# A decoder trunk's sums of the first gate and up weights formed during the second scan, and loads, casts and stores around the second norm in another order

## The chip, the cores and the metric

One core of a Trainium2 chip. The metric is the device time of one execution in microseconds, the lower the better. The engines are TensorE (PE: matmuls), VectorE (DVE), ScalarE (ACT), GpSimd (POOL) and SyncE (SP, which here only issues DMAs). Each works through its own instructions in program order and waits where an operand is not there yet.

## The reference

One layer of a hybrid decoder on x of 1024 rows by 1024 channels, in fp32:

```python
h = rms_norm(x, norm1_g)
proj = h @ w_in
o_a = gated_deltanet(q, k, v, z, a, b)   # 4 heads x 128, chunks of 64, a scan over the chunks
o_b = multiscale_pool(hp, pool_w, pool_scale)
o_c = short_gated_conv(cb, cc, ch, sconv_w)
x = x + concat(o_a, o_b, o_c) @ w_out
h = rms_norm(x, norm2_g)
ff = silu(h @ w_gate) * (h @ w_up)       # 2816 hidden channels
x = x + ff @ w_down
x = x + sigmoid(x @ ple_gate) * (p @ ple_proj)
return rms_norm(x, final_g)
```

## The kernel before

**Numbers as pairs.** An fp32 operand is split into a high part (a cast to fp32r on ACT) and a low part (operand minus high part, on DVE), and each product is three matmuls: high x high, high x low, low x high. Tiles are transposed: 128 channels on the partitions, 512 of the 1024 rows (a half, `hf`) along the free axis. A unit `u` is 128 x 512 fp32, 256 KB.

**Stages.** The input projection and the delta rule run for two pairs of heads. The scan of the second pair lies between some 260 and 370 us, with matmuls of the last input blocks filled in between its steps. The out-projection follows, half 0 from some 375 and half 1 from some 428 us: eight column blocks of `w_out` each, every block 512 KB, loaded into the buffer `wr`, cast into `wh` (ACT) and `wl` (DVE). For each block `out_evac` (L1233) adds the residual on DVE, squares on ACT, and adds to the sum of squares `ssq2` on DVE. `norm2` (L1266) then takes `rstd` (L457: four small matmuls of `ssq2` with `ones`, the scale `ms` on DVE, the power `rs` on POOL) and `rows` (L471: four diagonals on DVE, one product on PE that spreads them over the partitions), multiplies the tiles and splits them.

**Gate and up.** They are done two column blocks at a time by a Strassen form with seven products, whose right operands are the seven split sets `B[0]` to `B[6]` and whose left operands `op` are splits of weight blocks or of their sums. A sum takes four additions or subtractions for one weight pair. For the first four gemms (`EARLY`) they are made ahead: `early_sums` (L604) loads four units of a weight, makes four results on DVE and stores them in the scratch `sd_d`, from where `weights()` (L1340 and on) loads them later. For the others `sums(n)` (L1399) does it on POOL. `product` (L1470) runs the twelve matmuls of one product.

**Embedding.** `p_proc` (L1490) loads and splits the per-layer input `pT`, `embed` (L1512) multiplies it with `ple_proj` in sixteen banks of six matmuls, between the first products of gate and up, and `embed_evac` (L1504) copies each bank on ACT and stores it in the scratch `pp_d`, which is read at the end of the kernel.

**What sets the order.** A planner, `Flow` (L28), keeps modelled times. Each step is a generator that yields an event, a delay or both, and is resumed when the modelled time has come; what it then emits is appended to its engine's queue. Events and delays in the code thus fix the order of each engine's instructions, not when they run. `calm` lets a step wait until a modelled engine is nearly free. `op_slots` holds back the casts of `op`.

Of the kernel before, what the change touches and what calls it, by code (L numbers as in the profile page):

```python
# [24 lines left out]
EARLY = 4  # L25
# [171 lines left out]
def kernel(  # L197
# [19 lines left out]
    fl = Flow()  # L217
# [12 lines left out]
    pp_d = scr.tile([2, KT, P, HALF], F32, name="pp_d")  # L230
# [31 lines left out]
    def store(dst, src, ev):  # L262

        sync.dma_start(out=dst, in_=src)
        ev.set(2.6)
        yield 0
# [335 lines left out]
    sd_ev = [Event(fl) for _ in range(EARLY)]  # L602

    def early_sums():  # L604
        yield in_done[1], 8.0
        raw = []

        def fetch(n):
            raw.append([load(w[:, r]) for w in gate_up(n) for r in (slice(0, 4), slice(4, 8))])

        fetch(0)
        yield 5.0
        for n in range(EARLY):
            if n + 1 < EARLY:
                fetch(n + 1)
            a11, a12, a21, a22 = raw.pop(0)
            s1 = unit(shape=(P, 4, P))
            for out, in0, in1, op in ((s1, a21, a22, ALU.add), (a21, a11, a21, ALU.subtract),
                                      (a11, s1, a11, ALU.subtract), (a12, a12, a11, ALU.subtract)):
                yield from fl.calm(9, "vec", slack=0.5)  # L620
                vec.tensor_tensor(out=out, in0=in0, in1=in1, op=op)
            yield fl.left() + 1.0
            for i, t in enumerate((a11, a21, s1, a12)):
                sync.dma_start(out=sd_d[n, i // 2, :, 4 * (i % 2):4 * (i % 2) + 4], in_=t)
            a11 = a12 = a21 = a22 = s1 = t = None
            sd_ev[n].set(3.0)


    def conv_evac(tap, dst, ready):
# [359 lines left out]
    in_done = events(2)  # L989
# [239 lines left out]
    def xl_load(n):  # L1229
        if n < 2 * KT:  # L1230
            xl_.append(load(xT[n % KT, :, half(n // KT)]))
# [32 lines left out]
        B_ev[i][k].set(fl.left())  # L1264

    def norm2(hf, ts):  # L1266
        yield x1_ev[hf], 1.0 + 1.5 * hf
        rs = yield from rstd(ssq2[hf])
        ps = yield from rows(rs, unit())
        yield 0.3  # L1270

        def normed(j):
            t = ts[hf][j] = unit()
            vec.scalar_tensor_tensor(out=t, in0=x1[hf][j], scalar=vt[:, V_N2 + j:V_N2 + j + 1], in1=ps,
                                     op0=ALU.mult, op1=ALU.mult)
            x1[hf][j] = None
            return t

        if hf == 0:
            for j in range(KT):  # L1280
                t = normed(j)
                fl.spawn(b_split(j // 4, j % 4, t, vec), fl.left())
                yield fl.lag("vec")
            return
        T1, T2 = [None] * 4, [None] * 4
        for k in range(4):
            t12, t22 = normed(k), normed(4 + k)
            T1[k], T2[k] = unit(), unit()
            vec.tensor_tensor(out=T1[k], in0=t12, in1=ts[0][k], op=ALU.subtract)
            yield fl.lag("vec")  # L1290
            vec.tensor_tensor(out=T2[k], in0=t22, in1=T1[k], op=ALU.subtract)
            ts[0][k] = None
            fl.spawn(b_split(2, k, T2[k], vec), fl.left())
            yield fl.lag("vec")
        t2_ev.set()
        for k in range(4):
            t = ts[1][k]
            vec.tensor_tensor(out=t, in0=ts[1][4 + k], in1=t, op=ALU.subtract)
            fl.spawn(b_split(3, k, t, vec), fl.left())
            ts[1][k] = None  # L1300
            yield fl.lag("vec")
        for k in range(4):
            fl.spawn(b_split(4, k, T1[k], vec))
            T1[k] = None
            yield fl.lag("vec")
        for k in range(4):
            fl.spawn(b_split(5, k, ts[1][4 + k], vec))
            ts[1][4 + k] = None
            yield fl.lag("vec")
        b22_ev.set()  # L1310
        for k in range(4):
            t = ts[0][4 + k]
            vec.tensor_tensor(out=t, in0=t, in1=T2[k], op=ALU.subtract)
            fl.spawn(b_split(6, k, t, vec), fl.left())
            T2[k] = ts[0][4 + k] = None
            yield fl.lag("vec")
        t4_ev.set()
# [33 lines left out]
    def weights():  # L1351
# [45 lines left out]
                    yield 0.1  # L1397

        def sums(n):  # L1399
            yield raws[n][2]  # L1400
            yield raws[n][3]
            ra, rb = raws[n][0:2]
            a11, a12, a21, a22 = ra[:, 0:4], ra[:, 4:8], rb[:, 0:4], rb[:, 4:8]
            s1 = unit(shape=(P, 4, P))
            pool.tensor_tensor(out=s1, in0=a21, in1=a22, op=ALU.add)
            pool.tensor_tensor(out=a21, in0=a11, in1=a21, op=ALU.subtract)
            own[n] = (a11, a12, a11, a21, s1, a12, a22)
            yield split_ev[n]
            pool.tensor_tensor(out=a11, in0=s1, in1=a11, op=ALU.subtract)
            pool.tensor_tensor(out=a12, in0=a12, in1=a11, op=ALU.subtract)  # L1410
            yield fl.left()
            sum_ev[n].set()
# [77 lines left out]
    def p_proc(hf):  # L1490
        def ph():
            return unit(F32R) if hf else ffp.tile([P, HALF], F32R, tag="ph", name=nm("ph"), bufs=4)

        pH[hf] = [[ph() for _ in range(2)] for _ in range(2)]
        raw = [load(pT[k, :, half(hf)]) for k in range(2)]
        yield 4.0
        for k in range(2):
            hi, lo = pH[hf][k]
            act.copy(out=hi, in_=raw[k])
            yield fl.lag("act")  # L1500
            vec.tensor_tensor(out=lo, in0=raw[k], in1=hi.bitcast(F32), op=ALU.subtract)
            pH_ev[hf].set(fl.left())

    def embed_evac(ps, hf, j):  # L1504
        t = unit()
        act.copy(out=t, in_=ps)
        act.dma_start(out=pp_d[hf, j], in_=t)  # L1507
        free(ps)
        pp_ev[hf][j].set(4.0)
        yield 0  # L1510

    def embed(hf):  # L1512
        fl.until(pH_ev[hf])
# [125 lines left out]
    def down_sums(p, units=False):  # L1639
# [20 lines left out]
        if not units:  # L1660
            rb_slots.give()
            rb_slots.give()

    xl_load(0)
    ts2 = [[None] * KT, [None] * KT]
    for hf in range(2):
        fl.until(mix_done[hf])
        if hf == 1:
            ph1.close()
            ff = ctx.enter_context(ExitStack())  # L1670
            ffp = ff.enter_context(tc.tile_pool(name="ffp", bufs=2))
        fl.spawn(norm2(hf, ts2))
        for j in range(KT):
            w = wts.next()
            wts.prepare()
            if hf == 1 and j == 1:
                fl.spawn(weights())
                fl.spawn(p_proc(0), 12.0)
            ps = gemm(w, [mix[hf][k] for k in MIX_ORDER])
            fl.spawn(out_evac(ps, j, hf), 0.3)  # L1680
            if hf == 1 and j == KT - 2:
                out_w.set()
                for _ in range(4):
                    op_slots.give()


    x2 = [[None] * KT, [None] * KT]
# [48 lines left out]
            fl.spawn(down_sums(p), 2.0)  # L1736

    g = [t[1] for t in todo]
    fl.spawn(p_proc(1))
    for n in range(0, EARLY, 2):  # L1740
        for f in (Gemm.head1, Gemm.head2):
            f(g[n])
# [233 lines left out]
```

## Time and profile before

| | us |
|---|---|
| three runs | 1249.65, 1250.87, 1255.29 |
| median | 1250.87 |
| the profiled execution | 1251.02 |
| its span | 1249.2 |
| PE busy | 1214.4 (97%) |
| DVE busy | 812.4 (65%) |
| ACT busy | 530.3 (42%) |
| POOL busy | 295.3 (24%) |
| PE's mean granted clock | 0.991 |

Times in the trace count from the start of the span, which is 1.8 us shorter than the profiled execution. The granted clock is a share of the full 2.4 GHz; 0.50 is the lower of its two levels, 1.2 GHz. In a timeline, the bracket gives how long the engine idled before an instruction and what it had waited for, so the instruction's start less that time is where the wait began. L141 and L349 are helpers through which nearly all instructions of DVE, ACT and PE pass. The tile names are what tells them apart: `mm` and `dn` are banks of PSUM, `wr` raw weights, `wh`, `wl`, `op` split weights, `u` everything else of 128 x 512. The scratch `x1_d` appears as `x_d`.

### The profile page before, as it was taken

Reading aid. Unit: us, or ns where it says so; the run is one execution under the profiler, and the core shown is the slowest. Engines: PE = TensorE matmul, PEld = TensorE weight load, DVE = VectorE, ACT = ScalarE, POOL = GpSimd, SP = SyncE. Lnnn points to the kernel's source line nnn. Section 1 sums busy time; section 2 is a strip of 40 time slices with the busy share of each in tenths; the row PEclk is TensorE's granted clock in tenths of the full one; section 3 lists DMA queues with packets and bytes.
Section 4 is the critical chain, followed back from the end, with each engine's and each line's share of the span. In section 5 each row is a group of like instructions: output and inputs, shape, how many; then the busy total and the mean of one; then the engine's idle time right before and its main releaser. Section 6 shows DMA issues by size and latency. Waiting matters only on the chain.

```text
span 1249.2 us, 17275 instructions
## 1 busy us (share of the span) xinstructions
PE 1214.4 (97%) x6103; PEld 1002.4 (80%) x6103; DVE 812.4 (65%) x1397; ACT 530.3 (42%) x1114; POOL 295.3 (24%) x241
## 2 busy tenths in 40 slices
PE   8999999999999998999999999999999999999996
PEld 6778888888887776777888888888888888888886
DVE  8576785985767677685455657565655865553674
ACT  7255453244234243643333333333344644443553
POOL 7100001100010001013444658655733000000001
PEclk8999999999999999999999999999999999999998
DMA  6046353342245984543333546545569966563452
GB/s 224 18 136 188 110 132 98 108 110 86 86 158 205 325 288 152 181 157 110 110 110 127 177 136 223 180 134 171 177 227 375 323 221 199 178 194 112 147 181 94
DMA packets 119143, 208.18 MB, mean 167 GB/s; under 512 B 24400, under 2 KB 39568, under 8 KB 119056
## 3 DMA queue, kind: packets, MB, share of 16 engines
q1 hardware_dynamic: 116752, 202.88, 49.6%
q10 hardware_dynamic: 2304, 4.20, 0.9%
q8 instruction: 48, 0.79, 0.3%
q14 instruction: 39, 0.32, 0.1%
HBM read 148.53 MB, written 58.49 MB: 166 GB/s over the span
## 4 chain that ended last, share of the span: by engine, by line
PE 73%; DVE 5%; DMA 5%; ACT 3%; issue 2%; ACTq 0%; SPq 0%; POOL 0%; POOLq 0%; DVEq 0%
PE dn L349 44%; PE mm L349 28%; DVE u L141 3%; DMA wr<-in_w_out_dram 2%; ACT u L141 2%; PE dn L703 1%; DVE wl L141 1%; DVE op L141 1%; DMA wr<-in_ple_gate_dram 1%; DMA wr<-in_w_gate_dram 1%; ACT wh L141 1%; DMA sd_d<-u 1%; ACT op L141 0%; ACTq L1507 0%; DMA u<-in_pT_dram 0%
## 5 line engine op out<-in xcount | busy, mean ns | idle before, releaser
L349 PE MATMUL dn<-u,op 128*128 128x512 f32 x1632 | 375.4, 390 | 7.3 <-ACT u L141 4.2
L349 PEld LDWEIGHTS dn<-u,op 128*128 128x128 f32 x1632 | 305.9, 188 | 73.0 <-ACT u L141 5.5
L349 PE MATMUL mm<-u,wh 128*128 128x512 f32 x1104 | 356.4, 403 | 7.0 <-DVE u L141 5.7
L141 DVE TENSOR_TENSOR u<-u,u 128x512 fp32r<-128x512 f32 (+2 forms) x376 | 251.6, 702 | 63.7 <-ACT u L141 57.5
L349 PEld LDWEIGHTS mm<-u,wh 128*128 128x128 f32 x1104 | 202.9, 190 | 52.6 <-DVE u L141 8.4
L349 PE MATMUL mm<-u,wl 128*128 128x512 f32 x552 | 218.0, 395 | 0.9 <-DVE wl L141 0.9
L141 DVE TENSOR_TENSOR op<-wr,op 128x512 fp32r<-128x512 f32 x144 | 134.2, 936 | 104.1 <-ACT op L141 103.0
L141 ACT CAST u<-u 128x512 fp32r<-128x512 f32 x216 | 127.2, 621 | 139.1 <-DVE u L141 44.4
L349 PE MATMUL dn<-u,u 128*128 128x512 f32 (+2 forms) x850 | 159.4, 336 | 0.0
L349 PEld LDWEIGHTS dn<-u,u 128*128 128x128 f32 (+1 forms) x850 | 123.6, 170 | 24.0 <-issue 0.5
L141 ACT CAST op<-wr 128x512 fp32r<-128x512 f32 x144 | 88.4, 620 | 106.2 <-PE dn L349 60.3
L141 POOL TENSOR_TENSOR u<-u,u 128x512 f32<-128x512 f32 (+1 forms) x69 | 99.3, 1453 | 111.7 <-DVE u L141 80.5
L349 PEld LDWEIGHTS mm<-u,wl 128*128 128x128 f32 x552 | 104.8, 190 | 24.9 <-DVE wl L141 2.6
L141 ACT ACTIVATE u<-u 128x512 f32<-128x512 f32 (+1 forms) x137 | 82.1, 605 | 87.5 <-DVE u L141 86.0
L349 PE MATMUL mm<-u,u 128*128 128x512 f32 (+1 forms) x522 | 111.7, 351 | 2.1 <-DVE u L141 1.4
L141 DVE TENSOR_TENSOR wl<-wr,wh 128x512 fp32r<-128x512 f32 (+2 forms) x96 | 68.4, 714 | 65.2 <-ACT wh L141 64.5
L141 ACT COPY u<-dn 128x512 f32<-128x512 f32 (+4 forms) x99 | 47.7, 482 | 134.2 <-PE dn L349 121.1
L141 DVE TENSOR_TENSOR u<-dn,u 128x512 f32<-128x512 f32 x93 | 63.6, 688 | 58.5 <-PE dn L349 56.9
L349 PEld LDWEIGHTS mm<-u,u 128*128 128x128 f32 x522 | 85.5, 189 | 16.3 <-DVE u L141 2.0
L141 POOL TENSOR_TENSOR rs<-ms,mhalf 128x4 f32<-128x4 f32 (+1 forms) x7 | 7.0, 997 | 351.0 <-DVE ms L141 351.0
L141 ACT CAST wh<-wr 128x512 fp32r<-128x512 f32 (+2 forms) x96 | 57.7, 608 | 31.7 <-DMA wr<-in_w_out_dram 17.0
L349 PE MATMUL mm<-u,op 128*128 128x512 f32 x264 | 64.0, 391 | 2.0 <-ACT u L141 2.0
(164 smaller groups left out, 1103.9 us busy)
## 6 DMA issues: line engine op xcount, KB each, us to landing
a_d<-u SPq DMA_DIRECT2D x77, 256.0 KB, 2.9
u<-a_d SPq DMA_DIRECT2D x77, 256.0 KB, 3.9
u<-wd_d SPq DMA_DIRECT2D x44, 256.0 KB, 3.5
wr<-in_w_in_dram SPq DMA_DIRECT2D x21, 512.0 KB, 3.6
u<-in_w_down_dram SPq DMA_DIRECT2D x41, 256.0 KB, 4.9
wr<-in_w_gate_dram SPq DMA_DIRECT2D x20, 512.0 KB, 4.0
wr<-in_w_up_dram SPq DMA_DIRECT2D x20, 512.0 KB, 3.6
wr<-in_w_down_dram SPq DMA_DIRECT2D x18, 512.0 KB, 4.3
```

What stands on the lines that cost most here:

```text
L141: return f(*a, **kw)
L349: pe.matmul(out=out, lhsT=lhsT, rhs=rhs, start=start, stop=stop, **kw)
L703: pe.transpose(out=ps[:, t * P:(t + 1) * P], in_=src[:, t, :], identity=ident)
```

## The change

Six edits:

- `early_sums` starts when the first pair's scan is done, not 8 us (modelled) after the input projection, and loads the next weight's four units only 6 us after a weight's stores, not ahead of them. In the order of the instructions three of the four weights (12 sums, 12 loads, 12 stores) now stand inside the second pair's scan, the fourth in the out-projection's first half.
- `norm2` waits 4.0 instead of 1.0 after half 0's last square; half 1 keeps its 2.5.
- `sums(n)` of the first two POOL weights waits until `B[6]` is planned (`t4_ev`).
- `p_proc(1)` is started in the second half of the out-projection, not at the start of the products, `p_proc(0)` 2 us earlier; both wait 8 instead of 4 us for their loads.
- `embed_evac` stores through SP instead of ACT's queue, 16 stores.
- Four `op` slots are given when the last square is done (`more_slots`), not in the middle of the last block but one.

```diff
--- before.py
+++ after.py
@@ -602,7 +602,7 @@
     sd_ev = [Event(fl) for _ in range(EARLY)]
 
     def early_sums():
-        yield in_done[1], 8.0
+        yield scan_done[0]
         raw = []
 
         def fetch(n):
@@ -611,8 +611,6 @@
         fetch(0)
         yield 5.0
         for n in range(EARLY):
-            if n + 1 < EARLY:
-                fetch(n + 1)
             a11, a12, a21, a22 = raw.pop(0)
             s1 = unit(shape=(P, 4, P))
             for out, in0, in1, op in ((s1, a21, a22, ALU.add), (a21, a11, a21, ALU.subtract),
@@ -624,6 +622,10 @@
                 sync.dma_start(out=sd_d[n, i // 2, :, 4 * (i % 2):4 * (i % 2) + 4], in_=t)
             a11 = a12 = a21 = a22 = s1 = t = None
             sd_ev[n].set(3.0)
+            if n + 1 < EARLY:
+                yield 6.0
+                fetch(n + 1)
+                yield 6.0
 
 
     def conv_evac(tap, dst, ready):
@@ -1264,7 +1266,7 @@
         B_ev[i][k].set(fl.left())
 
     def norm2(hf, ts):
-        yield x1_ev[hf], 1.0 + 1.5 * hf
+        yield x1_ev[hf], 2.5 if hf else 4.0
         rs = yield from rstd(ssq2[hf])
         ps = yield from rows(rs, unit())
         yield 0.3
@@ -1397,6 +1399,8 @@
                     yield 0.1
 
         def sums(n):
+            if n < EARLY + 2:
+                yield t4_ev
             yield raws[n][2]
             yield raws[n][3]
             ra, rb = raws[n][0:2]
@@ -1493,7 +1497,7 @@
 
         pH[hf] = [[ph() for _ in range(2)] for _ in range(2)]
         raw = [load(pT[k, :, half(hf)]) for k in range(2)]
-        yield 4.0
+        yield 8.0
         for k in range(2):
             hi, lo = pH[hf][k]
             act.copy(out=hi, in_=raw[k])
@@ -1504,10 +1508,9 @@
     def embed_evac(ps, hf, j):
         t = unit()
         act.copy(out=t, in_=ps)
-        act.dma_start(out=pp_d[hf, j], in_=t)
         free(ps)
-        pp_ev[hf][j].set(4.0)
-        yield 0
+        yield fl.left() + 2.0
+        yield from store(pp_d[hf, j], t, pp_ev[hf][j])
 
     def embed(hf):
         fl.until(pH_ev[hf])
@@ -1661,6 +1664,11 @@
             rb_slots.give()
             rb_slots.give()
 
+    def more_slots():
+        yield x1_ev[1]
+        for _ in range(4):
+            op_slots.give()
+
     xl_load(0)
     ts2 = [[None] * KT, [None] * KT]
     for hf in range(2):
@@ -1675,13 +1683,13 @@
             wts.prepare()
             if hf == 1 and j == 1:
                 fl.spawn(weights())
-                fl.spawn(p_proc(0), 12.0)
+                fl.spawn(p_proc(0), 10.0)
+                fl.spawn(p_proc(1), 22.0)
             ps = gemm(w, [mix[hf][k] for k in MIX_ORDER])
             fl.spawn(out_evac(ps, j, hf), 0.3)
             if hf == 1 and j == KT - 2:
                 out_w.set()
-                for _ in range(4):
-                    op_slots.give()
+                fl.spawn(more_slots())
 
 
     x2 = [[None] * KT, [None] * KT]
@@ -1736,7 +1744,6 @@
             fl.spawn(down_sums(p), 2.0)
 
     g = [t[1] for t in todo]
-    fl.spawn(p_proc(1))
     for n in range(0, EARLY, 2):
         for f in (Gemm.head1, Gemm.head2):
             f(g[n])
```

Three places in the order of the instructions, of before and of the change.

DVE in the out-projection, at the end of half 0 and at the first norm: `u_3950` and `u_4009` are the sum of squares, `ms` and the diagonals (`ident,rs`) belong to `rstd` and `rows`. Before:

```order
L141 TENSOR_TENSOR wl_4287<-wr_4213,wh_4286 128x512
L141 TENSOR_TENSOR u_4290<-mm_4220,u_4230 128x512
L141 TENSOR_TENSOR wl_4287<-wr_4213,wh_4286 128x512
L141 TENSOR_TENSOR u_3950<-u_3950,u_4294 128x512
L141 TENSOR_TENSOR u_4144<-u_4144,u_4142 128x512
L141 TENSOR_TENSOR wl_4329<-wr_4270,wh_4328 128x512
L141 TENSOR_TENSOR u_4332<-mm_4282,u_4292 128x512
L141 TENSOR_SCALAR ms_4343<-dn_4338 128x4
L141 TENSOR_TENSOR wl_4329<-wr_4270,wh_4328 128x512
L141 TENSOR_SCALAR u_4372<-ident,rs_4345 128x128 x4
```

And now:

```order
L141 TENSOR_TENSOR wl_4301<-wr_4245,wh_4300 128x512
L141 TENSOR_TENSOR u_4304<-mm_4250,u_4260 128x512
L141 TENSOR_TENSOR wl_4301<-wr_4245,wh_4300 128x512
L141 TENSOR_TENSOR u_4009<-u_4009,u_4308 128x512
L141 TENSOR_TENSOR wl_4342<-wr_4286,wh_4341 128x512
L141 TENSOR_TENSOR u_4345<-mm_4296,u_4306 128x512
L141 TENSOR_TENSOR wl_4342<-wr_4286,wh_4341 128x512
L141 TENSOR_SCALAR ms_4379<-dn_4374 128x4
L141 TENSOR_SCALAR u_4391<-ident,rs_4381 128x128 x4
L141 TENSOR_TENSOR op_4396<-wr_4351,op_4396 128x512
```

The early sum `u_4144` is gone from here, and the second `wl` of the next block stands ahead of `ms`, where it stood between `ms` and the diagonals. On PE the four `rstd` matmuls stand 12 rows later, the product of `rows` 6 rows later, so that 12 instead of 18 matmuls lie between them.

ACT at the change from the out-projection to the products: `ACTIVATE u<-u` are squares, `op` casts of weights, `COPY u<-dn` the copies of the first products' banks, the casts of `pT`'s second half are `u_4733` and `u_4735` before, `u_4573` and `u_4575` now. Before:

```order
L141 CAST wh_4634<-wr_4577 128x512
L141 ACTIVATE u_4684<-u_4680 128x512
L141 CAST op_4686<-wr_4364 128x512
L141 CAST op_4694<-wr_4370 128x512
L141 CAST op_4700<-wr_4364 128x512
L141 CAST op_4709<-wr_4370 128x512
L141 ACTIVATE u_4743<-u_4741 128x512
L141 COPY u_4764<-dn_4729 128x512
L141 CAST u_4733<-u_4737 128x512
L141 CAST u_4735<-u_4739 128x512
L141 COPY u_4786<-dn_4760 128x512
L141 ACTIVATE u_4818<-dn_4729 128x512
```

And now:

```order
L141 CAST u_4573<-u_4577 128x512
L141 CAST wh_4641<-wr_4590 128x512
L141 CAST u_4677<-u_4646 128x512
L141 CAST u_4575<-u_4579 128x512
L141 ACTIVATE u_4699<-u_4695 128x512
L141 ACTIVATE u_4735<-u_4733 128x512
L141 COPY u_4752<-dn_4729 128x512
L141 CAST op_4754<-wr_4361 128x512
L141 CAST op_4760<-wr_4368 128x512
L141 CAST op_4766<-wr_4361 128x512
L141 CAST op_4784<-wr_4368 128x512
L141 COPY u_4794<-dn_4748 128x512
```

The four `op` casts move behind the last square and the first copy, and the two casts of `pT` ahead of the last two squares.

The embedding's stores: ACT before, with `COPY u<-mm` the copies of its banks:

```order
L141 COPY u_4950<-mm_4937 128x512
L1507 DMA pp_d<-u_4950 128x512
L141 COPY u_4960<-mm_4946 128x512
L1507 DMA pp_d<-u_4960 128x512
L141 CAST u_4964<-u_4928 128x512
L141 CAST op_4967<-wr_4435 128x512
L141 CAST op_4974<-wr_4435 128x512
L141 CAST u_4983<-u_4823 128x512
L141 COPY u_4986<-mm_4956 128x512
```

And SP now:

```order
L1375 DMA wr_4897<-sd_d 128x1024
L1375 DMA wr_4960<-sd_d 128x1024
L264 DMA pp_d<-u_4954 128x512
L1375 DMA wr_5006<-sd_d 128x1024
L264 DMA pp_d<-u_4973 128x512
L264 DMA pp_d<-u_4986 128x512
L264 DMA pp_d<-u_5000 128x512
L264 DMA pp_d<-u_5020 128x512
L264 DMA pp_d<-u_5031 128x512
L1375 DMA wr_5075<-sd_d 128x1024
L264 DMA pp_d<-u_5053 128x512
L264 DMA pp_d<-u_5065 128x512
```

The stores `pp_d` leave ACT's queue and stand on SP among the loads of `sd_d` and of the weights.

## Rows read from the trace of the kernel before

**Rows 1.** Page, part 1: engine, busy us (share of the span), number of instructions.

```profile
PE 1214.4 (97%) x6103; PEld 1002.4 (80%) x6103; DVE 812.4 (65%) x1397; ACT 530.3 (42%) x1114; POOL 295.3 (24%) x241
```

**Rows 2.** What PE waited for, 360 to 660 us: us in total, times, longest.

```profile
PE dn L349 <- DVE u L141: 4.1, 3, 2.0
PE dn L349 <- ACT u L141: 3.5, 2, 2.1
PE mm L349 <- ACT u L141: 2.4, 4, 0.9
...
PE mm L349 <- ACT wh L141: 0.5, 2, 0.3
```

**Rows 3.** Table by stretch: its length, each engine's busy us (instructions), clock, DMA share, GB/s.

```profile
280.00:300.00 20.00, 20.00 (x279) 16.57 (x279) 8.02 (x12) 10.28 (x25) 1.02 (x1) 1.00 0.36 108
420.00:440.00 20.00, 17.98 (x70) 14.32 (x68) 11.92 (x23) 5.81 (x10) 1.01 (x1) 0.83 1.00 355
...
431.65:438.50 6.85, 6.85 (x19) 5.54 (x20) 4.17 (x11) 1.76 (x3) 1.01 (x1) 0.50 0.98 310
438.52:445.30 6.78, 6.78 (x29) 5.26 (x28) 3.18 (x5) 1.76 (x3) 0.00 (x0) 1.00 1.04 414
```

**Rows 4.** Timeline of PE: start us, us, line, operation, count [idle before <- releaser].

```profile
376.48 0.50 PE L349 MATMUL mm<-u,wh 128*128 128x512 f32 x1 [0.92 <-DVE u L141]
...
431.13 1.42 PE L349 MATMUL dn<-ones,u 128*128 128x1 f32 x8 [2.02 <-DVE u L141]
...
483.06 0.96 PE L349 MATMUL dn<-u,op 128*128 128x512 f32 x3 [2.05 <-ACT u L141]
...
490.73 1.10 PE L349 MATMUL dn<-u,ones 128*128 128x512 f32 x2 [1.17 <-DVE u L141]
...
548.88 19.30 PE L349 MATMUL dn<-u,op 128*128 128x512 f32 x84 [2.15 <-ACT op L141]
```

**Rows 5.** Timeline of SP's queue (DMA issues), the same columns.

```profile
365.92 4.27 SPq L243 DMA_DIRECT2D u<-mx_d  x9
...
414.93 0.33 SPq L323 DMA_DIRECT2D wr<-in_w_out_dram  x1
...
418.14 3.74 SPq L624 DMA_DIRECT2D sd_d<-u  x4
...
543.39 0.93 SPq L1373 DMA_DIRECT2D wr<-sd_d  x2
```

**Rows 6.** Timeline of ACT.

```profile
421.60 0.62 ACT L141 CAST wh<-wr 128x512 fp32r<-128x512 f32 x1 [6.30 <-DMA wr<-in_w_out_dram]
...
482.44 0.57 ACT L141 COPY u<-dn 128x512 f32<-128x512 f32 x1
486.79 1.28 ACT L141 CAST u<-u 128x512 fp32r<-128x512 f32 x2 [3.78 <-DMA u<-in_pT_dram]
...
518.79 0.33 ACTq L1507 DMA_DIRECT2D pp_d<-u  x1
519.16 0.62 ACT L141 CAST op<-wr 128x512 fp32r<-128x512 f32 x1 [0.40 <-ACT u L141]
```

**Rows 7.** Timeline of DVE.

```profile
294.69 0.69 DVE L141 TENSOR_TENSOR u<-dn,cfv 128x512 f32<-128x512 f32 x1 [7.14 <-PE dn L703]
...
422.25 0.69 DVE L141 TENSOR_TENSOR wl<-wr,wh 128x512 fp32r<-128x512 f32 x1 [4.29 <-ACT wh L141]
...
435.94 0.87 DVE L141 TENSOR_SCALAR u<-ident,rs 128x128 f32<-128x128 f32 x4
...
475.97 4.70 DVE L141 TENSOR_TENSOR op<-wr,op 128x512 fp32r<-128x512 f32 x4 [1.21 <-ACT op L141]
```

**Rows 8.** Timeline of POOL.

```profile
434.27 1.01 POOL L141 TENSOR_TENSOR rs<-ms,mhalf 128x4 f32<-128x4 f32 x1 [59.26 <-DVE ms L141]
...
476.94 1.48 POOL L141 TENSOR_TENSOR u<-wr 128x512 f32<-128x512 f32 x1 [41.66 <-DMA wr<-in_w_gate_dram]
478.49 1.62 POOL L141 TENSOR_TENSOR wr<-wr,wr 128x512 f32<-128x512 f32 x1
```

## The prediction

> **What bounds the kernel now.** Read the page's busy line first: TensorE (PE) is busy 1214.4 of 1249.2 us [rows 1]. A change that adds no matmul can only return the idle 34.8 us and whatever a lower clock takes. The second view is therefore what PE waited for in the stretch that the diff touches, 360 to 660 us [rows 2]: 4.1 us in three waits for VectorE (DVE) on `dn` banks, 3.5 us in two for ScalarE (ACT), 2.4 us in four for ACT on `mm` banks, and 0.5 us for `wh`. The third view is the table by stretch [rows 3]. From 280 to 300 us, inside the second scan, PE is busy for 20.00 of 20 us while DVE works 8.02. From 420 to 440 us the DMA engines are busy the whole time (share 1.00, 355 GB/s), PE loses 2.02 us and its clock reads 0.83. The last two rows of that table narrow it down: from 431.65 to 438.50 PE never idles, but its clock is 0.50, and 19 matmuls fit where the next stretch of equal length at 1.00 holds 29. So one idle gap cost more than its own length. The timelines of single engines then say who was late.
>
> **The first norm's sum.** PE idled 2.02 us until 431.13 [rows 4], when the sum of squares for `rstd` arrived. Followed back: a `w_out` load issued at 414.93 stood among loads and `sd_d` stores [rows 5], and its cast began only at 421.60, after ACT had waited 6.30 us for the DMA [rows 6]. DVE then idled 4.29 us before the next `wl` [rows 7], and the sum stood behind that in its queue. The price was 2.02 us plus 6.85 us at half clock, half of which is lost: 2.02 + 3.43 = 5.45 us. The change acts twice. PE meets the `rstd` matmuls 12 matmuls later, 12 x 6.78 / 29 = 2.8 us by the last row of [rows 3], more than the 2.02 us missing. And the early sums leave: 12 of 16 loads and 12 of 16 stores, 256 KB each, 6.3 MB, or 18 us of DMA work at the 355 GB/s of [rows 3]. I take the whole 5.45 us. The 0.5 us on `wh` [rows 2] are late loads of the same stage, and go too.
>
> New here is a shorter cover for the next step. From `rstd` to `rows` there were 18 matmuls and are now 12, 2.8 us. In the trace the chain lasted from 431.13 to the end of the diagonals at 435.94 + 0.87 [rows 4, 7], 5.7 us, but at half clock and with one `wl` ahead of the diagonals on DVE; that `wl` now stands ahead of `ms`. What cannot shrink is the power on GpSimd (POOL), 1.01 us [rows 8], and the diagonals, 0.87. With the four small matmuls and `ms` I estimate 2.6 us. Bounds: 0 and 5.7 - 2.8 = 2.9 us of new idle. I take 0.3, near the low end, since DVE should come to `ms` some 4 us less late.
>
> **The early sums in the scan.** Twelve DVE sums of at most 0.69 us (the row at 294.69, [rows 7]) are 8.3 us, moved to a stage where that row shows DVE idle for 7.14 us in one piece. I cost them at nothing; the cover is that idle time and PE's other matmuls. They also bring 24 DMAs onto SyncE's (SP) queue. One place is tight: the `sd_d` stores of the third weight now stand ahead of the ten reloads of `mx_d`, whose issues began at 365.92 [rows 5], so these come later by up to 1 MB / 355 GB/s = 3 us. Their user is the out-projection's first gemm, where DVE already limits PE (0.92 us at 376.48, [rows 4]). Between 0 and 3 us I take 0.5, because the second half of the mix is read last.
>
> **The start of the products.** PE waited 2.05 us until 483.06 and 1.17 us until 490.73 [rows 4]; the two waits on ACT make 3.5 together [rows 2]. The first ended with the copy of bank `dn` at 482.44 [rows 6]. It stood behind the last square, which waited for DVE, and DVE had needed 4.70 us for four `op` subtractions at 475.97 [rows 7]. Four of 0.69 would be 2.8, so 1.9 us were lost, just where POOL ran its two weight sums of 1.48 and 1.62 us [rows 8]. The second wait: the copies stood behind two `pT` casts, for which ACT waited 3.78 us at 486.79 [rows 6]. The third is the second norm's `rows`, whose DVE steps stood behind the same subtractions of `pT`. The change takes each cause away in the order of the queues: `op` casts behind the first copy, POOL's sums behind both powers, and both `pT` casts ahead of the out-projection's last two squares. Gain 3.5 + 1.17 = 4.67 us; the low bound is 2.05, if only the reordered casts work.
>
> **The embedding.** Four waits for bank copies make 2.4 us [rows 2]. An issue of a `pp_d` store takes 0.33 us of ACT's queue at 518.79 and leaves a gap of 0.40 us before the next cast [rows 6], 16 times, 6.4 us in all. On SP they cost ACT nothing. Bounds 0 and 2.4; I take 2.4. The cost is on SP, where each store waits for its copy with `sd_d` and weight loads behind it.
>
> **What may grow.** At 548.88 PE waits 2.15 us, by the row for an `op` cast [rows 4]; the cast's `sd_d` load was issued only at 543.39 [rows 5]. Nothing in the change brings that forward for certain; it puts one more `op` subtraction ahead of the `dn` copy (0.7 us), and POOL's two sums now run just before it. The 1.9 us that DVE lost beside them fall partly into idle time. Between -2.15 and +3 I take +1.0.
>
> By the Trainium skill, SBUF - State Buffer, section "Who interferes with whom", a DVE instruction with two SBUF inputs contends with a GpSimd instruction that reads SBUF, and whichever started first blocks the other throughout. The 1.9 us lost beside POOL's sums agree with it in kind. By the rule the sums do not get cheaper by moving: DVE would lose up to the whole 3.1 us at the new place, and the time would be the second rival's.
>
> **Sum**, against the profiled execution's 1251.02 us (0.15 above the median of the runs): -5.45 - 0.5 - 4.67 - 2.4 + 0.3 + 0.5 + 1.0 = -11.2, so **1239.8 us**.
>
> **Rivals.**
> 1. The wait moves from `rstd` to `rows`. For: cover of 2.8 us against a chain that took 5.7, and `ms` behind a `wl` that needs a load in time. Against: DVE was late there only through that load. Price: 2.9 us, and the clock falls as it did: 2.9 + 3.43 - 0.3 = 6.0, so 1245.8 us. Chance 0.11.
> 2. POOL's sums block DVE in full at the new place, and stores on SP make the `op` load later. DVE loses 1.48 + 1.62 = 3.1 us in place of my 1.0, giving 1241.9; if the wait of then 5 us also brings the half clock, 3.4 more, 1245.3 us. For: the row at 475.97. Against: DVE has idle time there, and the 2.15 us so far cost no clock. Chance 0.12.
> 3. The change does not do what it says: other loads move up into the freed DMA time, loads stay late, and `rstd`'s wait with its clock, the `pT` wait and the `rows` wait remain. Only the reordered first copy (2.05) and the embedding (2.4) gain: 1246.6 us. For: share 1.00 leaves room for followers. Against: the 2.8 us of later demand need no DMA at all. Chance 0.09.
> 4. Slower: the sums in the scan. The scan is a chain from PE to DVE and back for each chunk, and a state update standing behind an early sum comes up to 0.69 us late. It decides if PE has no other matmul ready there. Then 12 x 0.69 = 8.3 us, and one fall of the clock for each of the three groups, 3 x 3.43 = 10.3: 1239.8 + 18.6 = 1258.4 us. For: sums are emitted in fours. Against: PE is busy for 20.00 of 20 us there [rows 3], so a late update finds other work. Chance 0.06.
>
> **How the numbers follow.** The forecast has 0.62. A measurement of this kernel tells about 0.5% or 6.25 us from no change, so faster means below 1244.6 us, slower above 1257.1. Faster: nearly all of the forecast (0.61), over half of the second rival (0.07) and the parts of the first that come with less idle (0.03), 0.71. Slower: the fourth, 0.06. Within 0.5%: the rest, 0.23. The low end: no new cost (13.0, 1238.0), the wait at 548.88 gone as well (1235.9), and an execution 1.4 below the profiled one, as the fastest of the runs is: 1234.5. The high end takes in the first three rivals with their 1246.6 and as much scatter: 1248.0. Left out are the fourth rival and a rest of the forecast, less than 0.2.
>
> **What would show it.** Right: PE never waits for `rstd`, its clock stays at 1.00 from 420 to 440 us, the DMA share there falls well below 1.00, no wait over 0.5 us from 480 to 492, four embedding waits gone and no `pp_d` on ACT; at about 549, less what was gained before it, a wait of 2 to 4 us stays. Wrong: a half clock anywhere between 360 and 560 us, PE waits inside the scan, or a wait of 3 us or more on `rows`, on the reloaded mix, or behind POOL's sums.

## The result, and the profile after

The changed kernel takes 1234.39 us (median of four runs, 1233.47 to 1234.97) against 1250.26 for the kernel before, measured along with it: 15.9 us less, a ratio of 0.9866 with an interval of 0.9837 to 0.9895. The profiled execution took 1234.97 us with a span of 1233.3; its clock is 0.995. The forecast of 1239.8 us had the direction right and was 5.4 us too high; its range ended at 1234.5, just above the measured median.

The page's busy line, to set beside [rows 1]:

```profile
PE 1209.9 (98%) x6103; PEld 1001.6 (81%) x6103; DVE 809.6 (66%) x1397; ACT 529.3 (43%) x1114; POOL 299.1 (24%) x241
```

PE's idle time fell from 34.8 to 23.4 us. What PE waited for from 340 to 640 us (the same stage as [rows 2]):

```profile
PE dn L349 <- DVE u L141: 1.6, 2, 0.9
PE mm L349 <- DVE u L141: 1.2, 2, 0.9
PE mm L349 <- DVE wl L141: 0.9, 1, 0.9
PE mm L349 <- ACT u L141: 0.7, 1, 0.7
```

Both waits of `dn` on ACT are gone, those on `wh` are gone, one of four bank waits is left. The single waits, PE's timeline with the columns of [rows 4]:

```profile
377.16 0.50 PE L349 MATMUL mm<-u,wh 128*128 128x512 f32 x1 [0.92 <-DVE u L141]
377.50 0.40 PE L349 MATMUL mm<-u,wl 128*128 128x512 f32 x1
377.73 0.39 PE L349 MATMUL mm<-u,wh 128*128 128x512 f32 x1
378.37 0.50 PE L349 MATMUL mm<-u,wh 128*128 128x512 f32 x1 [0.24 <-DVE u L141]
378.71 0.40 PE L349 MATMUL mm<-u,wl 128*128 128x512 f32 x1
...
388.47 0.50 PE L349 MATMUL mm<-u,wl 128*128 128x512 f32 x1 [0.90 <-DVE wl L141]
...
432.35 0.95 PE L349 MATMUL dn<-ones,u 128*128 128x1 f32 x8
...
436.02 1.02 PE L349 MATMUL dn<-u,ones 128*128 128x512 f32 x2
...
514.34 1.65 PE L349 MATMUL mm<-u,op 128*128 128x512 f32 x6 [0.69 <-ACT u L141]
...
532.94 3.44 PE L349 MATMUL dn<-u,op 128*128 128x512 f32 x14 [0.63 <-DVE u L141]
...
553.18 7.08 PE L349 MATMUL dn<-u,op 128*128 128x512 f32 x30 [0.93 <-DVE u L141]
```

The `rstd` matmuls at 432.35 and `rows` at 436.02 run without a wait, the diagonals between them on DVE ending in time; so does the whole start of the products.

```profile
433.33 0.16 DVE L141 TENSOR_SCALAR ms<-dn 128x4 f32<-128x4 f32 x1 [0.52 <-PE dn L349]
434.62 0.88 DVE L141 TENSOR_SCALAR u<-ident,rs 128x128 f32<-128x128 f32 x4 [1.12 <-POOL rs L141]
```

The table by stretch, as [rows 3]:

```profile
420.00:440.00 20.00, 20.00 (x92) 16.32 (x91) 10.23 (x21) 8.58 (x15) 1.01 (x1) 1.00 0.77 280
480.00:500.00 20.00, 20.00 (x90) 16.53 (x89) 19.77 (x32) 10.51 (x20) 0.00 (x0) 1.00 0.21 70
```

PE is busy for 20.00 us in both, the clock is 1.00, and the DMA share in the first fell from 1.00 to 0.77. One place went the other way than forecast: the wait that was 2.15 us at 548.88 is 0.63 us at 532.94.

**Where the 15.9 us come from.** Span against span, by the idle times: `rstd` with its half clock 5.45, `wh` 0.55, start of the products 4.68, embedding 2.35 - 0.69 = 1.66, the later `op` 2.15 - 0.63 = 1.52. That makes 13.9. The first wait of the out-projection stands at 377.16 where it stood at 376.48, so 0.7 was lost ahead of it; the same matmuls are 0.7 us apart in the two traces from 30 us on, so all of it arose in the first 30 us and none in the scan. The rest, 15.9 - 13.9 + 0.7 = 2.7 us, lies in no idle time that a row shows.

The first rows above tell how a wait can cost more than its bracket: the wait at 378.37 is given as 0.24 us, but matmuls start at 377.73, 378.37 and 378.71, 0.64 and 0.34 us apart, where they are 0.23 apart without a wait. So that wait cost 0.52 us. The bracket counts from the end of the row before, 0.39 us after its start, though without a wait the next matmul would have started 0.23 us after it.

The start of the same matmul in both traces tells where the 2.7 us lie. Four such pairs, PE's timeline, before:

```profile
457.09 0.39 PE L349 MATMUL mm<-u,wl 128*128 128x512 f32 x1
...
475.40 0.84 PE L349 MATMUL dn<-u,op 128*128 128x512 f32 x3
...
504.61 7.76 PE L349 MATMUL mm<-ph,op 128*128 128x512 f32 x33
...
530.25 1.07 PE L349 MATMUL dn<-u,op 128*128 128x512 f32 x4
```

And now:

```profile
452.31 0.39 PE L349 MATMUL mm<-u,wl 128*128 128x512 f32 x1
...
469.40 0.84 PE L349 MATMUL dn<-u,op 128*128 128x512 f32 x3
...
493.09 7.64 PE L349 MATMUL mm<-ph,op 128*128 128x512 f32 x33
...
515.83 0.39 PE L349 MATMUL dn<-u,op 128*128 128x512 f32 x1
```

The change is 0.7 us behind at the first norm, then 4.8, 6.0, 11.5 and 14.4 us ahead in these pairs, and 15.9 at the later `op` (548.88 and 532.94). So the stages gained:

| | by idle time and clock, us | by the starts, us |
|---|---|---|
| the first norm | 5.45 | 5.5 |
| the two waits on `wh` | 0.55 | 1.2 |
| the start of the products | 4.68 | 5.5 |
| the embedding | 1.66 | 2.9 |
| the later `op` | 1.52 | 1.5 |

The 1.2 of the second row is 1.7, less 0.5 that the change lost just behind, at 460.8 to 461.9 us, in starts 0.34 to 0.39 us apart before which no idle time is shown. The 2.7 us are thus the short waits' surcharge; for the nine waits that went (twelve from 388 to 570 us before, three now) it is 0.3 us on average, none of it at the first norm or the later `op`.

### The profile page after: what moved, and what is told of

It reads as the page before. It is cut to its first block, busy times and chain, and to the rows that moved or that the text cites. A ratio compares the mean times of both kernels' runs of the same rounds, so it can differ in the third digit from the quotient of the medians.

```text
span 1233.3 us, 17272 instructions
## 1 busy us (share of the span) xinstructions
PE 1209.9 (98%) x6103; PEld 1001.6 (81%) x6103; DVE 809.6 (66%) x1397; ACT 529.3 (43%) x1114; POOL 299.1 (24%) x241
## 4 chain that ended last, share of the span: by engine, by line
PE 89%; DVE 5%; DMA 3%; issue 1%; ACT 1%; SPq 0%; POOLq 0%; POOL 0%; DVEq 0%; ACTq 0%
PE dn L349 47%; PE mm L349 41%; DVE u L141 3%; PE dn L705 1%; ACT u L141 1%; DMA u<-mx_d 1%; DMA u<-in_xT_dram 1%; DMA wr<-in_ple_gate_dram 1%; DVE op L141 1%; DMA wr<-in_w_in_dram 0%; ACT op L141 0%; DMA pp_d<-u 0%; DMA wr<-sd_d 0%; DVE wl L141 0%; DVE pol L141 0%
## 5 line engine op out<-in xcount | busy, mean ns | idle before, releaser
L141 DVE TENSOR_TENSOR op<-wr,op 128x512 fp32r<-128x512 f32 x144 | 130.3, 910 | 99.7 <-ACT op L141 98.7
L141 DVE TENSOR_TENSOR u<-mm,u 128x512 f32<-128x512 f32 x60 | 41.2, 687 | 35.4 <-PE mm L349 34.5
```

What stands on the lines that cost most here:

```text
L141: return f(*a, **kw)
```

## The experiments

All times are medians; the changed kernel's is 1234.39. Each group of runs had the kernel before measured along with it, at 1249.35 to 1250.33 us, so a difference of less than 1 us between groups tells nothing. Theory A in each is the forecast's reading of that place, in the light of the trace after.

### The first norm: data or demand

Runs e1 to e3 undo the early sums, the first norm's delay, and both.

```diff
 def early_sums():                          # e1, e3
-    yield scan_done[0]
+    yield in_done[1], 8.0
...
+        if n + 1 < EARLY:
+            fetch(n + 1)
...
-        if n + 1 < EARLY:
-            yield 6.0
-            fetch(n + 1)
-            yield 6.0
 def norm2(hf, ts):                         # e2, e3
-    yield x1_ev[hf], 2.5 if hf else 4.0
+    yield x1_ev[hf], 1.0 + 1.5 * hf
```

> The changed kernel with the early sums where they were before (in the out-projection); all else as changed. Theory A (the later demand alone covers the first norm's sum: 2.8 us later against the 2.02 missing): no wait on rstd, clock 1.00 from 420 to 440 us, only late w_out loads come back, 0.5 us in two waits and about 0.3 more for each; 1235.5 us. Rival B (the freed DMA time is what counts): the rstd wait and its half clock come back, 5.5 us and more; 1240 us or above. Rival C (the wait moves to the rows product, whose cover is shorter): 1 to 3 us on rows, with half clock up to 6; 1236 to 1240 us.

> The changed kernel with the old delay in the first norm (rstd's matmuls 12 rows earlier again); the early sums stay in the scan. Theory A (either edit alone is enough): the sum is ready some 4 us earlier than before, no wait on rstd, clock 1.00; 1234.4 us, no difference. Rival B (the delay is what counts): a wait on rstd of 0.5 to 2 us, with half clock 1 to 5.5 us; 1235.5 to 1240 us.

> The changed kernel with the early sums and the first norm's delay both as before; the other four edits stay. Theory A: the rstd wait of 2 us and the half clock of 6.9 us come back, with the two waits on wh, 5.45 + 0.5 and about 0.3 for each of three waits: +6.8 us, 1241.2 us. Rival (the wait depended on the other edits too): less than 3 us, below 1237.5 us.

Measured: e1 1238.57, e2 1234.22, e3 1238.55 us. With the sums back, PE's timeline and the table by stretch (e1):

```profile
438.01 1.94 PE L349 MATMUL dn<-u,ones 128*128 128x512 f32 x2 [2.55 <-DVE u L141]
...
420.00:440.00 20.00, 17.45 (x75) 13.55 (x75) 12.50 (x23) 6.30 (x11) 1.38 (x1) 0.95 1.01 363
440.00:460.00 20.00, 20.00 (x86) 16.46 (x86) 15.03 (x24) 10.62 (x20) 0.00 (x0) 0.96 0.91 333
```

Rival C held: the later demand covers `rstd`, but the wait moves to `rows`, 2.55 us, with part of the half clock (0.95 and 0.96). In e3 the wait is on `rstd` again, 0.97 us and a clock of 0.91, and the time the same; theory A had put it 2.6 us higher. The delay alone changes nothing in either pair (e2 against the change, e3 against e1). What a late `w_out` load costs, and where, also differs from one execution to the next: e12 below has the instructions of the kernel before in the same order up to the start of the products, but its profile shows 0.74 us on `rstd` and a clock of 1.00 from 420 to 440 us, and four waits on `wh`, one on `wl` and one on `rows` instead of two on `wh`. By the matmul starts it ran this stage only 1.0 us faster.

The sums brought two loads back at once, 7.4 us of DVE and 6.3 MB of DMA. Runs e5 and e6 add one of them to the changed kernel.

```diff
+def dummy_dma():                           # e5
+    yield in_done[1], 8.0
...
+        for i, (w, r) in enumerate(...):
+            sync.dma_start(out=dm_d[n, 4 * c + i], in_=w[:, r])
...
+def dummy_dve():                           # e6
+    yield in_done[1], 8.0
+    t, o = load(gate_up(0)[0][:, 0:4]), unit(shape=(P, 4, P))
...
+    for n in range(3):
+        for _ in range(4):
...
+            vec.tensor_tensor(out=o, in0=t, in1=t, op=ALU.add)
```

> The changed kernel plus 24 copies of 256 KB from the weights to an unread scratch in DRAM, issued on SyncE about where the early sums' loads and stores were before (6.3 MB); the computation is unchanged. Theory A (it was the DMA time that made the first norm late): w_out loads late again, 2 to 6 us of ScalarE waiting for one, a wait of 1 to 3 us on rstd or rows of the first norm, with its half clock; 1237 to 1240 us. Rival B (it was VectorE's twelve sums): no wait there, within 1 us of the changed kernel, 1234.4 us.

> The changed kernel plus twelve unread additions of 128 x 512 on VectorE about where the early sums stood before (7.4 us of VectorE), and one load. Theory A (DMA time): VectorE has over 6 of 20 us idle there; no wait on rstd or rows, 1234.4 us. Rival B (VectorE's time): a wait of 1 us or more on rstd or rows, 1236 to 1240 us.

Measured: e5 1240.18, e6 1233.63 us. The table by stretch for the changed kernel, then for e5, then for e6:

```profile
400.00:440.00 40.00, 40.00 (x180) 32.90 (x179) 22.23 (x39) 14.50 (x25) 1.01 (x1) 1.00 0.77 265
```

```profile
400.00:440.00 40.00, 38.45 (x167) 30.04 (x166) 20.67 (x36) 12.42 (x22) 1.01 (x1) 1.00 0.99 353
```

```profile
400.00:440.00 40.00, 40.00 (x180) 32.72 (x179) 28.73 (x49) 15.25 (x27) 1.38 (x1) 1.00 0.76 266
```

And what ACT waited for in e5 (in the changed kernel no cast of that stretch waits for a `w_out` load):

```profile
ACT wh L141 <- DMA wr<-in_w_out_dram: 11.6, 5, 3.4
```

DVE 28.73 us busy instead of the change's 22.23 cost nothing; a DMA share of 0.99 cost 5.8 us. By the matmul starts, e5 loses 4.5 us against e6 between 386 and 466 us and 0.2 us behind that. So DMA traffic alone is enough to make the stage late, and DVE's sums alone are not. The form was a little different from what theory A said: four short waits on `wh` and one of 0.55 us on `rows`, no half clock. (The later `op` wait, 1.97 us in e5, is 1.65 in e6 too, so it is not the copies' doing.) The loads themselves show it: the median time from issue to landing of the sixteen `w_out` loads is 4.9 to 5.9 us in the five profiles with that traffic in the out-projection (before, e1, e3, e5, e12) and 3.9 to 4.1 in the other thirteen. The copies also take SP's time to issue, four of them 2.4 to 3.1 us; how much of the 5.8 us comes from that is not separated.

### The embedding's stores

Run e4 puts the stores back on ACT; e12 is the kernel before with that edit alone, e11 with the early sums alone.

```diff
 def embed_evac(ps, hf, j):                 # e4; reversed in e12
...
+    act.dma_start(out=pp_d[hf, j], in_=t)
     free(ps)
-    yield fl.left() + 2.0
-    yield from store(pp_d[hf, j], t, pp_ev[hf][j])
...
```

> The changed kernel with the sixteen embedding stores back on ScalarE's queue. Theory A (ScalarE's 6.4 us of issues make both the bank waits and the later wait for an op): three more waits in the embedding, together 1.7 us of idle and about 0.3 more each, and the wait after the B[6] splits grows from 0.63 to some 2 us: +4 us, 1238.4 us. Rival B (the later wait shrank for another reason, as the loads of sd_d or the sums on GpSimd): only the embedding's part, +2.5 us, 1236.9 us, and that wait stays at 0.6 us.

> The kernel before with only the early sums moved into the second scan. Theory A (they took the DMA time that made the first norm late): no wait on rstd, no half clock at 431 us, no wait on wh: 5.45 + 0.5 + 0.3 to 0.5 for each of three waits, about 7 us less, 1243 us; the waits at the start of the products and in the embedding stay. Rival B (other edits are needed for that): less than 4 us, above 1246 us.

> The kernel before with only the embedding's stores on SyncE. Theory A: the four waits of the embedding shrink to one of 0.7 us and the wait at the later op from 2.15 to about 1: 1.7 + 1.2 and 0.3 to 0.5 for each of three waits, 4 us less, 1246 us. Rival B (ScalarE is the bound there with or without the issues, or SyncE's stores hold its loads): less than 2 us, above 1248 us.

Measured: e4 1238.86, e11 1244.12, e12 1245.44 us. In e4 three bank waits are back (1.93 us together), and the later one grew, PE's timeline:

```profile
536.10 4.18 PE L349 MATMUL dn<-u,op 128*128 128x512 f32 x12 [3.14 <-ACT op L141]
```

So ACT's 6.4 us of issues made both: theory A. How the issues reach the later wait stands on SP's queue, the change and then e4:

```profile
526.14 2.13 SPq L1375 DMA_DIRECT2D wr<-sd_d  x2
```

```profile
529.02 1.53 SPq L1375 DMA_DIRECT2D wr<-sd_d  x2
```

These loads need buffers that earlier `op` splits give back (`rb_slots`). In the change they are issued 6.2 us before PE begins to wait for the later `op` (532.94 - 0.63), in e4 3.9 us (536.10 - 3.14), in the kernel before 3.3 us (543.39 and 548.88 - 2.15, [rows 4, 5]). e11 and e12 came out within about 1 us of theory A's figures. Against the kernel before measured along with them, 1249.35 us, they gain 5.2 and 3.9 us, near what e1 and e4 lose, 4.2 and 4.5; in e12 the later `op` wait fell to 1.09 us. The forecast had priced the embedding alone. By the Trainium skill, DMA: Bandwidth & Descriptors, section "Issuing engines are not separate DMA queues", a DMA runs on the same 16 engines whoever starts it, and starting it elsewhere saves only the time on the sequencer, which the page calls usually small. Here that time, sixteen times 0.40 us on ACT, cost the kernel 4.5 us, since what PE waited for stood behind it.

### The start of the products

Undone one at a time from the changed kernel: the hold on GpSimd's sums (e7), the late op slots (e9), the early `pT` (e10). In e8 the hold is 8 us longer.

```diff
 def sums(n):                               # e7, e8
-    if n < EARLY + 2:
-        yield t4_ev                        # e8: yield t4_ev, 8.0
...
 if hf == 1 and j == KT - 2:                # e9
...
-    fl.spawn(more_slots())
+    for _ in range(4):
+        op_slots.give()
...
-fl.spawn(p_proc(0), 10.0)                  # e10, and the delay 4.0
-fl.spawn(p_proc(1), 22.0)
+fl.spawn(p_proc(0), 12.0)
...
+fl.spawn(p_proc(1))
```

> The changed kernel with GpSimd's sums of the first two weights no longer held back, so that they stand ahead of the second norm's power and run beside the first op subtractions, as before; the other edits stay. Theory A (each reordering at the start of the products counts by itself): the second norm's rows product waits for its power, which stands behind up to 3.1 us of sums, 1 to 2 us; the first copies, now ahead of the op casts, do not wait; 1236 us. The wait at the later op (0.63 us) stays within 1 us of that. Rival B (the early casts and the late op slots are enough): no wait between 470 and 490 us, 1234.4 us or less.

> The changed kernel with GpSimd's sums of the first two weights another 8 us (modelled) later, behind the B[6] splits. In the changed kernel the first sum took 4.82 us on GpSimd beside VectorE's splits, against 1.3 us elsewhere. Theory A (whoever starts first keeps the other out): no sum beside the splits, none stretched, VectorE not held; the wait of 0.63 us for an op stays or goes; 1233.8 to 1234.4 us. Rival B (the sums are then late for weight 4's ops): a new wait of 1 us or more between 545 and 575 us, 1235.5 to 1237 us.

> The changed kernel with the four op slots given in the last block but one again, so that the first op casts and subtractions stand ahead of the last squares and the first copy; the other edits stay. Theory A (the copy's wait of 2.05 us came from the subtractions stretched beside GpSimd's sums): GpSimd's sums are elsewhere now, the subtractions take 2.5 us together, the first copy waits 0 to 0.7 us; 1234.4 to 1235 us. Rival B (the casts' place ahead of the square is enough): a wait of 1.5 to 2 us at the first copy, 1236.5 us.

> The changed kernel with the second half of the per-layer input loaded at the start of the products again and the old delays; the other edits stay. Theory A (the two casts that wait for their loads hold the next copy): the wait of 1.5 us comes back, and with it the one on the second norm's rows, 1.2 us, together 2.7 and 0.3 to 0.5 for each; 1237.5 us. Rival B (the loads land in time, since the early sums' stores no longer stand behind them): below 1 us, 1235 us.

Measured: e7 1234.03, e8 1233.46, e9 1234.19, e10 1233.02 us. None has a wait between 465 and 490 us. In e8 GpSimd's first sums ran at 522.07, no later than in its neighbours, so it tells nothing of its question. No single edit is needed: e9 is theory A's figure, e7 and e10 are rival B's. The next four therefore start from the two edits with an effect and add one.

> Only two of the six edits: the early sums in the scan and the embedding's stores on SyncE. Theory A (the waits at the start of the products need one of the other edits): 1.5, 1.5 and 1.2 us there, as in the run with the sums alone, and 0.3 to 0.5 for each: 1234.4 + 5.5, 1239 to 1240 us. Rival B (they go when the stage before and the embedding no longer crowd them): below 1236.5 us.

> Three of the six edits: those two and the four op slots given after the last square. Theory A (the late slots alone clear the start of the products: the first copy ahead of the casts, and the loads of pT ahead of those of ple_proj on SyncE): no wait between 465 and 490 us, 1233 to 1234.5 us, so that the first norm's delay, the held sums and the early pT are worth nothing. Rival B (the held sums or the early pT are needed too): 1236 us or more.

> Three of the six edits: those two and GpSimd's sums held back. Theory A (the first copy waited only because the subtractions ran beside GpSimd's sums): the first wait falls from 1.5 to below 0.5 us, those behind the pT casts, 1.5 and 1.2, stay: 1237 to 1238 us. Rival B (the casts ahead of the square are the cause): the first wait stays, 1239 us or more.

> Three of the six edits: those two and the early loads of pT. Theory A: the wait behind the pT casts and the one on rows go, the first copy's 1.5 us stays: 1235.5 to 1236.5 us. Rival B (the first wait alone delays the power and the rows too): 1238 us or more.

Measured: e13 1240.70, e14 1233.58, e15 1239.21, e16 1236.83 us. The early sums alone (e11) show the causes unmixed. DVE's four subtractions beside GpSimd's two sums, and PE's waits that follow:

```profile
466.89 4.69 DVE L141 TENSOR_TENSOR op<-wr,op 128x512 fp32r<-128x512 f32 x4 [1.21 <-ACT op L141]
```

```profile
473.98 0.96 PE L349 MATMUL dn<-u,op 128*128 128x512 f32 x3 [1.49 <-ACT u L141]
...
479.44 0.96 PE L349 MATMUL dn<-u,op 128*128 128x512 f32 x3 [1.53 <-ACT u L141]
481.59 2.04 PE L349 MATMUL dn<-u,ones 128*128 128x512 f32 x2 [1.18 <-DVE u L141]
```

With the sums held (e15) the same four take 2.50 us, and PE's first wait is gone, but ACT's `pT` casts still wait for their loads and PE waits behind them:

```profile
467.31 2.50 DVE L141 TENSOR_TENSOR op<-wr,op 128x512 fp32r<-128x512 f32 x4 [1.21 <-ACT op L141]
```

```profile
477.32 1.28 ACT L141 CAST u<-u 128x512 fp32r<-128x512 f32 x2 [5.17 <-DMA u<-in_pT_dram]
```

```profile
479.14 0.97 PE L349 MATMUL dn<-u,op 128*128 128x512 f32 x3 [2.54 <-ACT u L141]
481.25 2.05 PE L349 MATMUL dn<-u,ones 128*128 128x512 f32 x2 [1.14 <-DVE u L141]
```

In e16 the loads come early: the second and third waits go, and the first stays, 2.56 us at 475.38. The late slots do both at once (e14): the first copy stands ahead of the `op` casts, and, since the `op` splits free the buffers that the `ple_proj` loads need, those loads are issued later and the `pT` loads stand ahead of them on SP. SP's queue, e14 and then e15:

```profile
464.87 0.95 SPq L243 DMA_DIRECT2D u<-in_pT_dram  x2
...
473.35 0.89 SPq L1372 DMA_DIRECT2D wr<-in_ple_proj_dram  x2
```

```profile
469.23 1.92 SPq L1372 DMA_DIRECT2D wr<-in_ple_proj_dram  x4
...
471.70 0.91 SPq L243 DMA_DIRECT2D u<-in_pT_dram  x2
```

e13, e14 and e16 are within 0.7 us of theory A's figures; e15 is 1.2 above, since its second wait grew to 2.54 us and the clock fell to 0.91 from 480 to 500 us. So three of the six edits, at 1233.58 us, are the whole gain: early sums, late slots, stores on SP. The first norm's delay, the held sums and the early `pT` are worth nothing beside them. The late slots are one way of two: in e9 they are undone, and with the other three edits in place of them no wait comes back. e14 and e10 are 0.8 and 1.4 us below the changed kernel, less than what a measurement here can tell from no change.

## Why the prediction was right or wrong

- **The first norm's sum, 5.45 and 0.5:** the 5.45 was right in size and cause; e5 and e6 show that DMA traffic is enough to make the sum late. The 0.5 was too low, the matmul starts show 1.2. "The change acts twice" was wrong: the later demand is worth nothing by itself, it only moves the wait to `rows` (e1), which was the first rival's mechanism.
- **The cover for `rows`, +0.3:** it cost nothing. From the `rstd` matmuls at 432.35 to the end of the diagonals at 434.62 + 0.88 it took 3.2 us, more than the estimate of 2.6, but the cover was 3.7, since it also holds the four small matmuls.
- **The early sums in the scan, 0 and +0.5:** no wait in the scan, and the three waits of the out-projection's start are the same 0.92, 0.24 and 0.90 us as before. The fourth rival had no ground.
- **The start of the products, 4.67:** the idle time is as forecast, the gain 5.5. The causes are the ones named (e11, e15, e16), but the forecast took each edit to be needed for its own wait. The late slots clear all three.
- **The embedding, 2.4:** 1.66 of its idle time went, one wait of 0.69 is left. By the starts it gained 2.9.
- **"Between -2.15 and +3 I take +1.0":** this step failed. It measured -1.52, 2.5 us on the other side. "Nothing in the change brings that forward for certain" overlooked that ACT's 6.4 us in the embedding, freed in the part just before, let everything after it on ACT run ahead of PE, the `op` casts whose splits give back the buffers of the `sd_d` loads among it; e4 shows it, with 3.14 us when the issues return. The wait is shorter in all profiles: 0.53 to 1.97 us in the fifteen with the stores on SP, 2.04 to 3.14 in the three with them on ACT. The size of 1.52 is in part luck, since GpSimd's sums fell so that they did not hold DVE (below); in e2, where they did and the clock fell to 0.91, this place took 1.3 us more than before by the matmul starts.
- **What no term had, and this step failed too:** the sum took a wait's price from the idle time in its bracket alone. The surcharge, 0.3 us on average for nine waits, makes 2.7 us. With -1.52 in place of +1.0 the forecast is 1237.3, with the surcharge also 1234.6. Of the two only the surcharge explains why the median lies below the range: its low end of 1234.5 already had the later `op` wait gone, and with the surcharge it would have been 1231.8.
- **The second rival**, GpSimd's sums holding DVE at their new place, did not come in the changed kernel's profile, where the sums were held themselves. In e2, e5, e6 and e8 it did come, in part: DVE lost up to 2.1 us and PE waited 1.47 to 1.97 us at the later `op`, far from the 5 us that the rival put there.

## What to carry to other kernels

Where transfers saturate the DMA engines in one stage and a neighbour stage leaves them idle, moving whole blocks of work there is worth more than any delay in the late consumer: the delay only moves the wait on. When time is given back to an engine, look at what stands next in its queue and carry the gain on to the next wait, not only to the waits it was meant for. Several edits against one wait can each be enough: undo them in pairs, or start from the kernel before, since undoing one at a time shows nothing. Price a wait by the starts of the instructions around it and not by its idle time alone: here the idle times left out 2.7 of 15.9 us.

## What the runs showed of the hardware

Two sums on GpSimd beside additions on DVE: one of the two engines is held, and it is not always the same. In the changed kernel GpSimd's sum took 4.82 us, where it takes 1.3 in other places, and DVE ran on without a gap:

```profile
524.85 4.82 POOL L141 TENSOR_TENSOR u<-wr 128x512 f32<-128x512 f32 x1 [47.40 <-DMA pp_d<-u]
```

```profile
524.83 1.29 DVE L141 TENSOR_TENSOR op<-wr,op 128x512 fp32r<-128x512 f32 x2
...
526.63 1.89 DVE L141 TENSOR_TENSOR op<-wr,op 128x512 fp32r<-128x512 f32 x3
```

In e2, the same place and the same instructions, GpSimd kept its 1.3 us and DVE lost 2.06 us in two subtractions, 3.35 in place of 1.29, and PE's wait there was 1.90 us instead of 0.63:

```profile
521.51 0.69 DVE L141 TENSOR_TENSOR u<-dn,u 128x512 f32<-128x512 f32 x1
522.11 3.35 DVE L141 TENSOR_TENSOR op<-wr,op 128x512 fp32r<-128x512 f32 x2
```

```profile
521.92 1.29 POOL L141 TENSOR_TENSOR u<-wr 128x512 f32<-128x512 f32 x1 [47.07 <-DMA pp_d<-u]
523.29 1.62 POOL L141 TENSOR_TENSOR wr<-wr,wr 128x512 f32<-128x512 f32 x1
```

By the Trainium skill, SBUF - State Buffer, section "SBUF: two separate sides", whichever starts first of a DVE instruction with two SBUF inputs and a GpSimd instruction that reads SBUF blocks the other for a whole instruction. The rows agree: in the changed kernel DVE's subtraction started 0.02 us before GpSimd's sum, and in e2 the sum started while DVE ran an addition that reads a PSUM bank (`dn`). They add that GpSimd can be held for several instructions in a row: e15 (6.07 us for the sum) and e10 (6.49) are like the changed kernel. Eleven profiles have the first sum beside DVE's work at this place. In the five where the DVE instruction at its start, or the next, read a `dn` bank, it took 1.29 to 1.68 us (e2, e4, e5, e6, e8); in the six where neither did, 3.83 to 6.49 (the change, e1, e3, e9, e10, e15). This is not the whole rule: at the start of the products, as in e11 above, GpSimd's sums came in between two subtractions that read no PSUM bank.

A wait does not always bring the half clock: 2.05 us at 483.06 [rows 4] left it at 1.00, 2.02 at 431.13 did not. In the runs, 2.55 us (e1) cost some 1.8 us of clock over two stretches, 1.90 us (e2) left 0.91 in its stretch, and 1.97 us (e5) left 1.00. What decides it was not tried. Lastly, PE comes to the wait of 0.9 us at the out-projection's start between 374.6 and 377.2 us in these profiles. That spread is all there after the first 30 us, and between 200 and 386 us the same matmul's lead over the kernel before changes by at most 0.1 us in any of them, whether the early sums run in the scan or not. A single profile is better compared from there on.
